# Attention in a two-layer backbone step: order of transposes and value products, and the split of PSUM banks between them

## The chip, the cores and the metric

The kernel runs on 1 core of one Trainium2 chip. The metric is device time of one execution in microseconds; the median of three runs is given, with the lowest and the highest. TensorE is called PE in the profile, its weight loads PEld, VectorE DVE, ScalarE ACT, GpSimd POOL, and SP issues DMAs.

## The reference

One inference step of a backbone with two layers works on 1024 latent tokens (a grid 64 wide) and 256 context tokens of 1024 channels. Layer 0 has neighbourhood attention (8 heads of 64) beside a pooling mixer, layer 1 windowed attention with grouped keys (16 query heads, 4 key heads) and a learned sink per head; each layer ends in a SwiGLU mixer. Cut to the windowed attention:

```python
qb = (q * hd ** -0.5).reshape(bsz, nb, C_BLOCK, hkv, g, hd)
s_nb = jnp.einsum('bnqkgd,bnjkd->bnkgqj', qb, kband)        # 3 blocks of 128 keys, banded
s_nb = jnp.where(valid, s_nb, NEG_INF)
s_ctx = jnp.einsum('bnqkgd,bpkd->bnkgqp', qb, k_ctx)        # 512 cached context keys
p = jax.nn.softmax(jnp.concatenate([sl, s_ctx, s_nb], axis=-1), axis=-1)   # sl: the sink
out = (jnp.einsum('bnkgqp,bpkd->bnqkgd', p[..., 1:1 + n_ctx], v_ctx)
       + jnp.einsum('bnkgqj,bnjkd->bnqkgd', p[..., 1 + n_ctx:], vband))
```

The neighbourhood attention has the same form with a learned bias per offset in place of the band, and no sink. Context tokens attend densely to the 256 context tokens.

## The kernel before, in words

The attention of both layers is one function, `attention` (from L619), called once per layer. Its work is a list of units. A unit is one head and 128 queries with all their keys: 896 keys in layer 0, 896 or 768 in layer 1 (the first and the last block of queries has one block of keys fewer). Units come in pairs a, a+1: the two heads that share a 128-row tile of queries and keys. Per head pair there are eight such long pairs and, after the fourth, one short pair for the context tokens (512 columns: two blocks of 128 queries with 256 keys each). Layer 0 has 4 head pairs, layer 1 has 8.

A unit goes through these steps:

- scores (L632, PE): three products per piece of keys for both heads in turn, into `ps_s`, a tile of two PSUM banks, of which there are two;
- `least` (DVE, L646, or L640 to L643 for short units): adds bias or mask, takes the minimum of the negated logits, and writes `sP` in SBUF;
- `exps` (ACT, L652 and L660): exponentials and their sum, with one more small one for the sink;
- `total` (DVE, L666 and L667): adds the sink term and takes the reciprocal;
- `normalise` (POOL or DVE, L674): scales `sP`;
- `transposes` (PE, L684): 128x128 blocks of `sP` into `ps_t`, four to a bank, so two groups for a long unit;
- `evacuate` (ACT L689 or DVE L691): each group from PSUM to `sT` (`sR` for short units);
- `values` (PE, L700): `sT` times V for both heads side by side, into one bank of `ps_o`;
- `out`: `mix_out` splits the output into a high part (ACT, L1346) and then a low part (DVE, L1348), after which the bank of `ps_o` is free.

PSUM has eight banks here: four for `ps_s`, two for `ps_t`, two for `ps_o`.

The order is written by a planner, `Order`, before anything is emitted. All PE steps are chained by `in_turn`, so PE runs them in just the order in which the loop at the end of `attention` adds them. The steps of the other engines are placed by a greedy list schedule with written costs: among the steps whose predecessors are planned it takes the one that could start earliest, and between equal starts the one of lower class. `least`, `exps` and `total` have class 0, `normalise` and `evacuate` 1, the bias tiles and the two halves of `out` 2. Where a step may go on two engines, it takes the one on which it would end first. A step that takes a slot (`s`, `t`, `o`, `P`, `T`, `R` for the tiles above) can only be planned when a slot has been given back. What the planner emits is fixed: each engine then works through its queue in that order.

DMA loads of keys, queries and values, and some background work, are emitted with the scores.

Of the kernel before, what the change touches and what calls it, by code (L numbers as in the profile page):

```python
# [9 lines left out]
F32 = mybir.dt.float32  # L10
# [113 lines left out]
def hybrid_step(ctx: ExitStack, tc: tile.TileContext, I: dict, O: list):  # L124
# [494 lines left out]
    def attention(p, us, NP, NT, NR, NB, lag, early, spare, bias_ns, lead):  # L619
        psS, c1 = attn_psum  # L620
        NU = len(us)
        S, P, M, T, B, PO = {}, {}, {}, {}, {}, {}
# [53 lines left out]
        def transposes(u, lo, hi):  # L676
            nb = us[u].nb
            if lo == 0:
                T[u] = (p.tile([128, 896], F32, name="sT", bufs=NT) if nb == 1 else
                        p.tile([128, 512], F32, name="sR", bufs=NR))  # L680
            pt = T[u, lo] = psS.tile([128, 512], F32, name="ps_t", bufs=2)
            for i in range(lo, hi):
                j = i // nb + us[u].n // 128 // nb * (i % nb)
                pe.transpose(pt[:, 128 * (i - lo):128 * (i - lo) + 128], P[u][:, 128 * j:128 * j + 128], ident)  # L684

        def evacuate(u, lo, hi, e):
            o, i = T[u][:, 128 * lo:128 * hi], T.pop((u, lo))[:, 0:128 * (hi - lo)]
            if e is act:
                act.activation(o, i, AF.Copy)  # L689
            else:  # L690
                dve.tensor_copy(o, i)  # L691

        def values(a, b, j0, j1, last):
            if j0 == 0:
                PO[a] = psS.tile([128, 512], F32, name="ps_o", bufs=2)
            v = [us[u].vs() for u in (a, b)]
            w = 128 * us[a].nb
            for j in range(j0, j1):
                for h, u in enumerate((a, b)):
                    pe.matmul(PO[a][64 * h:64 * h + 64, 0:w], v[h][j], T[u][:, w * j:w * j + w],  # L700
                              start=(j == 0), stop=(j == len(v[0]) - 1))
            if last:
                T.pop(a), T.pop(b)

        o = Order(lag, s=2, b=NB, P=NP, t=2, T=NT, R=NR, o=2)
        tail = [None]
        ev, ready, queue = {}, {}, []

        def in_turn(on, emit, after, take=(), give=()):
            r = tail[0] = o.add((0, 0), {pe: on}, emit, list(after) + ([tail[0]] if tail[0] else []), take, give)  # L710
            return r

        def issue(a):
            g = us[a]
            n, nb = g.n, g.nb
            own = g.bias is not None and g.sink is None
            sc = in_turn(n * 15 // 11 + 170, lambda e: scores(a), [], ["s", "s"])
            for u in (a, a + 1):
                g, on = us[u], []
                if own:  # L720
                    on = [o.add((2, u), {pool: bias_ns}, lambda e, u=u, g=g: B.update({u: g.bias()}), take=["b"])]
                elif g.bias is not None:
                    B[u] = g.bias()
                here = ["P"] if g.bias is not None else []
                on = o.add((0, u), {dve: n * 11 // 10 + 200}, lambda e, u=u: least(u), [sc] + on, here,
                           (["b"] if own else []) + (["s"] if here else []))
                on = o.add((0, u), {act: n * 5 // 6 + 200 + 144 * (nb - 1) + (0 if g.sink is None else 190)}, lambda e, u=u: exps(u),
                           [on], [] if here else ["P"], [] if here else ["s"])
                on = o.add((0, u), {dve: 160 if g.sink is None else 250}, lambda e, u=u: total(u), [on])
                ready[u] = o.add((1, u), {dve: n * 11 // 20 + 60 * nb} if u < early else  # L730
                                 {pool: n + lead * nb, dve: n * 11 // 20 + spare * nb}, lambda e, u=u: normalise(u, e), [on])

        def turn(u):
            nch = us[u].n // 128
            ev[u] = []
            for lo in range(0, nch, 4):
                hi = min(lo + 4, nch)
                w = 128 * (hi - lo)
                tr = in_turn(107 * (hi - lo) + 30, lambda e, lo=lo, hi=hi: transposes(u, lo, hi), [ready[u]],
                             ["t"] if lo else ["TR"[us[u].nb - 1], "t"], ["P"] if hi == nch else [])  # L740
                ev[u].append(o.add((1, u), {act: 50 + w * 5 // 6, dve: 64 + w * 21 // 20},
                                   lambda e, lo=lo, hi=hi: evacuate(u, lo, hi, e), [tr], give=["t"]))

        def combine(a):
            b, nb, nj = a + 1, us[a].nb, us[a].n // 128 // us[a].nb
            cuts = [0, 4, nj] if nj > 4 else [0, nj]
            for j0, j1 in zip(cuts, cuts[1:]):
                last = j1 == nj
                pv = in_turn((5 + 215 * nb) * (j1 - j0) + 80, lambda e, j0=j0, j1=j1, last=last: values(a, b, j0, j1, last),
                             ev[a] + ev[b], [] if j0 else ["o"], ["TR"[nb - 1]] * 2 if last else [])  # L750
            hi = o.add((2, b), {act: 50 + 110 * nb}, lambda e: us[a].out(0, PO[a]), [pv])
            o.add((2, b), {dve: 70 + 130 * nb}, lambda e: us[a].out(1, PO.pop(a)), [hi], give=["o"])

        for a in range(0, NU + 6, 2):
            if a < NU:
                issue(a)
            if 2 <= a < NU + 2:
                turn(a - 2)
            if 4 <= a < NU + 4:
                combine(a - 4)  # L760
            if 2 <= a < NU + 2:
                turn(a - 1)
        o.run()


# [371 lines left out]
    for ti in (1, 2):  # L1137
        o, n = TB[ti]
# [275 lines left out]
    for hp in range(4):  # L1414
# [28 lines left out]
        for h in range(2):  # L1443
# [10 lines left out]
            us_p.append(Unit(2 * PROMPT, segs, vs, out, nb=2))  # L1454
        us += interleave(us_l, us_p)
    attention(p, us, 4, 4, 2, 3, 80, 3, 1000, 950, 100)
    bg.flush()
    attn_psum[1]()
# [99 lines left out]
    for gi, size in enumerate((4, 2, 2, 2, 2)):  # L1558
# [3 lines left out]
        for ti in range(3):  # L1562
            for (kind, i), (wi, w) in zip(grp, ws):
                pt = ps_tile()
# [44 lines left out]
    for c in range(8):  # L1609
# [27 lines left out]
        for h in range(2):  # L1637
# [10 lines left out]
            us_p.append(Unit(2 * PROMPT, segs, vs, out, nb=2, sink=lambda h=h, c=c: sinkt[:, 2 * c + h:2 * c + h + 1]))  # L1648
        us += interleave(us_l, us_p)
    attention(p, us, 6, 4, 2, 0, 80, 3, 1000, 450, 100)  # L1650
    bg.flush()
    attn_psum[1]()
# [69 lines left out]
```

## Time and profile before

| | us |
|---|---|
| median of 3 runs | 3088.11 |
| lowest, highest | 3081.44, 3091.46 |
| profiled execution | 3094.04 |
| its span, first to last instruction | 3092.3 |
| PE busy | 2937.8 (95%) |
| PEld, DVE, ACT, POOL busy | 2489.7, 1875.6, 1089.3, 822.8 |
| granted PE clock, mean | 0.975 of full speed |

The attention of layer 0 lies at about 298 to 495 us of the span, that of layer 1 at 1728 to 2072. The rest is dense products. An engine's busy time says how long it worked and not whether anything waited for it; a wait is read from the start of an instruction and from the releaser that the trace puts beside it.

### The profile page before, as it was taken

The numbers are of one execution on the slowest core, as the hardware profiler recorded it, in microseconds if no ns is written. First come the engines' busy times: TensorE is split into PE (matmuls) and PEld (weight loads), VectorE is DVE, ScalarE is ACT, GpSimd is POOL, SyncE is SP. The second block draws the span as 40 slices with busy tenths as digits, with TensorE's granted clock in tenths as the row PEclk, the third lists the DMA queues.
The fourth block names the chain that finished last, engine by engine and source line by source line (L and its number), as shares of the span: only waits on it lengthen the run. The fifth ranks groups of instructions, "written<-read, shape, count | busy, mean of one in ns | idle before, by whom it ended". The sixth has DMA issues, their size and how long they took to land.

```text
span 3092.3 us, 46174 instructions
## 1 busy us (share of the span) xinstructions
PE 2937.8 (95%) x18074; PEld 2489.7 (81%) x18074; DVE 1875.6 (61%) x3035; ACT 1089.3 (35%) x2084; POOL 822.8 (27%) x692
## 2 busy tenths in 40 slices
PE   6999999988999999899999999999789999999998
PEld 4878777867888887788878777878678888888887
DVE  5654665577777776544455688862767555554334
ACT  4233773343333332000332577761433333330002
POOL 0241542232333332000222344431323333320002
PEclk9999999989999999999999999999899999999999
DMA  6467644213434436543133410123033223255421
GB/s 248 146 194 228 154 128 154 89 49 129 136 127 130 133 126 237 203 172 138 68 122 141 154 59 31 36 83 99 24 130 116 92 93 101 102 180 204 177 102 69
DMA packets 184330, 394.55 MB, mean 128 GB/s; under 512 B 32176, under 2 KB 69424, under 8 KB 177840
## 3 DMA queue, kind: packets, MB, share of 16 engines
q1 hardware_dynamic: 180656, 385.34, 36.7%
q0 software_dynamic: 3456, 6.26, 0.8%
q8 instruction: 143, 2.34, 0.3%
q14 instruction: 75, 0.61, 0.1%
HBM read 274.32 MB, written 118.23 MB: 127 GB/s over the span
## 4 chain that ended last, share of the span: by engine, by line
PE 68%; DVE 11%; ACT 5%; issue 3%; POOL 3%; DMA 2%; SPq 0%; DVEq 0%; ACTq 0%; POOLq 0%
PE psd L1063 6%; PE psd L1065 6%; PE psd L1064 6%; PE psd L307 6%; PE psd L309 6%; PE psd L308 6%; PE psd L884 6%; PE psd L885 6%; PE psd L886 6%; PE ps_t L684 5%; PE ps_o L700 5%; PE ps_s L632 4%; DVE nacc L388 2%; ACT whl L280 2%; DVE whl L282 2%
## 5 line engine op out<-in xcount | busy, mean ns | idle before, releaser
L308 PE MATMUL psd<-A,whl 128*128 128x256 f32 (+1 forms) x1760 | 585.9, 333 | 16.0 <-DVE A L490 15.0
L307 PE MATMUL psd<-A,whl 128*128 128x256 f32 (+1 forms) x1760 | 588.9, 335 | 7.3 <-ACT A L454 2.7
L309 PE MATMUL psd<-A,whl 128*128 128x256 f32 (+1 forms) x1760 | 583.1, 331 | 2.0 <-DVE whl L282 2.0
L280 ACT ACTIVATE whl<-wraw 128x1024 fp32r<-128x1024 f32 x178 | 187.1, 1055 | 649.7 <-PE psd L1065 461.2
L1063 PE MATMUL psd<-A,whl 128*128 128x512 f32 (+1 forms) x1056 | 378.1, 358 | 16.3 <-DVE x L1067 10.3
L308 PEld LDWEIGHTS psd<-A,whl 128*128 128x128 f32 x1760 | 341.6, 194 | 52.5 <-DVE A L490 17.5
L1064 PE MATMUL psd<-A,whl 128*128 128x512 f32 (+1 forms) x1056 | 376.1, 356 | 0.0
L1065 PE MATMUL psd<-A,whl 128*128 128x512 f32 (+1 forms) x1056 | 376.0, 356 | 0.0
L307 PEld LDWEIGHTS psd<-A,whl 128*128 128x128 f32 x1760 | 342.2, 194 | 41.3 <-ACT A L454 3.2
L309 PEld LDWEIGHTS psd<-A,whl 128*128 128x128 f32 x1760 | 346.0, 197 | 31.7 <-DVE whl L282 3.3
L1067 DVE SCALAR_TENSOR_TENSOR x<-psd,modv,x 128x512 f32<-128x512 f32 (+1 forms) x288 | 186.9, 660 | 283.1 <-PE psd L1065 278.8
L282 DVE TENSOR_TENSOR whl<-wraw,whl 128x1024 fp32r<-128x1024 f32 x174 | 238.7, 1374 | 145.4 <-ACT whl L280 143.3
L884 PE MATMUL psd<-A,whl 128*128 128x512 f32 x704 | 277.4, 394 | 0.0
L885 PE MATMUL psd<-A,whl 128*128 128x512 f32 x704 | 275.4, 391 | 0.0
L886 PE MATMUL psd<-A,whl 128*128 128x512 f32 x704 | 275.4, 391 | 0.0
L674 POOL TENSOR_SCALAR sP<-sP,sm 128x896 f32<-128x896 f32 (+2 forms) x206 | 179.4, 875 | 245.8 <-DVE sm L667 120.0
L1063 PEld LDWEIGHTS psd<-A,whl 128*128 128x128 f32 x1056 | 201.1, 190 | 45.5 <-DVE x L1067 11.1
L1065 PEld LDWEIGHTS psd<-A,whl 128*128 128x128 f32 x1056 | 202.1, 191 | 28.0
L1064 PEld LDWEIGHTS psd<-A,whl 128*128 128x128 f32 x1056 | 201.1, 190 | 27.6
L684 PE MATMUL ps_t<-ident,sP 128*128 128x128 f32 x1408 | 206.6, 285 | 7.3 <-POOL sP L674 2.6
L426 POOL TENSOR_TENSOR nacc<-nacc,ec 128x512 f32<-128x512 f32 (+1 forms) x32 | 34.7, 1084 | 623.2 <-ACT ec L425 621.8
L684 PEld LDWEIGHTS ps_t<-ident,sP 128*128 128x128 f32 x1408 | 152.8, 143 | 57.3 <-issue 24.5
(224 smaller groups left out, 5246.6 us busy)
## 6 DMA issues: line engine op xcount, KB each, us to landing
hd<-x SPq DMA_DIRECT2D x84, 512.0 KB, 3.1
A<-hd SPq DMA_DIRECT2D x20, 2048.0 KB, 12.3
wraw<-in_w_gu_dram SPq DMA_DIRECT2D x60, 512.0 KB, 3.6
st<-in_w_mod_dram SPq DMA_DIRECT2D x112, 256.0 KB, 2.8
wraw<-in_w_down_dram SPq DMA_DIRECT2D x44, 512.0 KB, 3.7
wrawx<-in_w_gu_dram SPq DMA_DIRECT2D x28, 512.0 KB, 3.7
A<-hd SPq DMA_DIRECT2D x14, 1024.0 KB, 14.8
wmod<-in_w_mod_dram SPq DMA_DIRECT2D x48, 256.0 KB, 3.0
```

The lines of the kernel that those rows point to most:

```text
L280: act.activation(h[:, 0], src, AF.Copy)
L282: eng.tensor_tensor(h[:, 1], src, h[:, 0].bitcast(F32), op=OP.subtract)
L307: pe.matmul(ps[:, :n], wh, A[ti].part(0, k), start=(k == 0), stop=False)
L308: pe.matmul(ps[:, :n], wh, A[ti].part(1, k), start=False, stop=False)
L309: pe.matmul(ps[:, :n], wl, A[ti].part(0, k), start=False, stop=(k == 7))
L684: pe.transpose(pt[:, 128 * (i - lo):128 * (i - lo) + 128], P[u][:, 128 * j:128 * j + 128], ident)
L884: pe.matmul(pt, wh, t(0, c), start=(c == 0), stop=False)
L885: pe.matmul(pt, wh, t(1, c), start=False, stop=False)
L886: pe.matmul(pt, wl, t(0, c), start=False, stop=(c == 3))
L1063: pe.matmul(pt[:, :n], wh, t[:, 0, k], start=(k == 0), stop=False)
L1064: pe.matmul(pt[:, :n], wh, t[:, 1, k], start=False, stop=False)
L1065: pe.matmul(pt[:, :n], wl, t[:, 0, k], start=False, stop=(k == nk - 1))
```

## The change

The loop that adds the steps puts the transposes of both heads of a pair side by side and the value products after them. Before, the value products stood between the two heads' transposes. With it `ps_t` gets three banks in place of two and `ps_o` one in place of two; the planner is told the same numbers.

```diff
-            pt = T[u, lo] = psS.tile([128, 512], F32, name="ps_t", bufs=2)
+            pt = T[u, lo] = psS.tile([128, 512], F32, name="ps_t", bufs=3)
...
-                PO[a] = psS.tile([128, 512], F32, name="ps_o", bufs=2)
+                PO[a] = psS.tile([128, 512], F32, name="ps_o", bufs=1)
...
-        o = Order(lag, s=2, b=NB, P=NP, t=2, T=NT, R=NR, o=2)
+        o = Order(lag, s=2, b=NB, P=NP, t=3, T=NT, R=NR, o=1)
...
         for a in range(0, NU + 6, 2):
             if a < NU:
                 issue(a)
             if 2 <= a < NU + 2:
                 turn(a - 2)
+                turn(a - 1)
             if 4 <= a < NU + 4:
                 combine(a - 4)
-            if 2 <= a < NU + 2:
-                turn(a - 1)
         o.run()
```

## Rows read from the trace of the kernel before

**Rows 1.** The page: an engine's busy us, share, instructions; then the chain by engine.
```profile
PE 2937.8 (95%) x18074; PEld 2489.7 (81%) x18074; DVE 1875.6 (61%) x3035; ACT 1089.3 (35%) x2084; POOL 822.8 (27%) x692
...
PE 68%; DVE 11%; ACT 5%; issue 3%; POOL 3%; DMA 2%; SPq 0%; DVEq 0%; ACTq 0%; POOLq 0%
```

**Rows 2.** Busy time by stretch: start:end, us, engines, granted clock, DMA share, GB/s.
```profile
core 0: us, PE busy (x) PEld busy (x) DVE busy (x) ACT busy (x) POOL busy (x), PEclk, DMA share, GB/s
337.60:341.00 3.40, 3.40 (x29) 3.07 (x30) 0.27 (x1) 0.10 (x1) 0.94 (x1) 0.50 0.02 5
443.15:448.10 4.95, 4.95 (x56) 4.05 (x55) 3.57 (x9) 4.05 (x9) 2.88 (x4) 1.00 0.02 3
1811.80:1854.08 42.28, 41.90 (x449) 33.67 (x449) 34.62 (x96) 32.93 (x90) 17.67 (x21) 1.00 0.19 77
1825.56:1844.08 18.52, 18.39 (x192) 14.45 (x192) 15.76 (x43) 13.76 (x39) 7.94 (x10) 1.00 0.00 1
```

**Rows 3.** Timeline, weight loads of layer 1: start, us, engine, line, count [idle before <-releaser].
```profile
1818.56 1.29 PEld L700 LDWEIGHTS ps_o<-sT,V 128*64 128x64 f32 x24 [0.16 <-issue]
...
1825.56 1.17 PEld L632 LDWEIGHTS ps_s<-Ka,Qa 64*128 64x128 f32 x12 [0.17 <-DVE sm L666]
...
1826.98 0.75 PEld L684 LDWEIGHTS ps_t<-ident,sP 128*128 128x128 f32 x7 [0.25 <-POOL sP L674]
...
1827.89 1.51 PEld L700 LDWEIGHTS ps_o<-sT,V 128*64 128x64 f32 x28 [0.17 <-issue]
...
1829.57 0.75 PEld L684 LDWEIGHTS ps_t<-ident,sP 128*128 128x128 f32 x7 [0.17 <-issue]
...
1830.49 0.77 PEld L632 LDWEIGHTS ps_s<-Ka,Qa 64*128 64x128 f32 x12 [0.17 <-DVE sm L667]
```

**Rows 4.** Timeline, from scores to the second head's normalisation; a 768-key pair first.
```profile
1811.80 1.11 PEld L632 LDWEIGHTS ps_s<-Ka,Qa 64*128 64x128 f32 x12 [0.17 <-issue]
...
1817.65 0.91 POOL L674 TENSOR_SCALAR sP<-sP,sm 128x768 f32<-128x768 f32 x1 [0.39 <-DVE A L1348]
...
1820.83 1.51 PE L632 MATMUL ps_s<-Ka,Qa 64*128 64x512 f32 x12
...
1823.56 1.15 DVE L646 CUSTOM_DVE_ANT_0 sP<-ps_s,maskc,sinkt 128x896 f32<-128x896 f32 x1
...
1825.10 0.27 ACT L1346 ACTIVATE A<-ps_o 128x128 fp32r<-128x128 f32 x1
...
1825.44 1.05 ACT L660 ACTIVATE sP<-sP,sm 128x896 f32<-128x896 f32 x1
...
1827.20 1.01 POOL L674 TENSOR_SCALAR sP<-sP,sm 128x896 f32<-128x896 f32 x1 [0.39 <-DVE A L1348]
```

**Rows 5.** Timeline, ACT: an evacuation ahead of the second head's exponentials.
```profile
1801.78 0.59 ACT L689 ACTIVATE sT<-ps_t 128x512 f32<-128x512 f32 x1
...
1802.25 0.30 ACT L652 ACTIVATE sm<-sinkt,sm 128x1 f32<-128x1 f32 x1
```

**Rows 6.** Timeline near short pairs of layer 1.
```profile
1799.86 1.08 PE L700 MATMUL ps_o<-sR,V 128*64 128x256 f32 x8
...
1831.64 0.67 DVE L640 TENSOR_REDUCE sm<-ps_s 128x2 f32<-128x512 f32 x1
...
1832.48 1.75 PE L700 MATMUL ps_o<-sT,V 128*64 128x128 f32 x28
...
1834.97 0.27 DVE L1348 TENSOR_TENSOR A<-ps_o,A 128x128 fp32r<-128x128 f32 x1
...
1836.95 0.42 PEld L684 LDWEIGHTS ps_t<-ident,sP 128*128 128x128 f32 x4 [0.25 <-POOL sP L674]
```

**Rows 7.** DVE's evacuations in layer 1 by tile: count, ns min/median/max, first and last start.
```profile
L691 DVE COPY sT<-ps_t x88: 411/670/692, 1735.5 to 2069.8; 128x512 f32<-128x512 f32 x46, 128x384 f32<-128x384 f32 x32, 128x256 f32<-128x256 f32 x10
```

**Rows 8.** Timeline of layer 0, from scores to the second head's normalisation.
```profile
441.73 1.49 PE L632 MATMUL ps_s<-Kb,Qb 64*128 64x512 f32 x12
...
447.30 1.02 POOL L674 TENSOR_SCALAR sP<-sP,sm 128x896 f32<-128x896 f32 x1 [0.81 <-DVE sm L667]
```

**Rows 9.** Timeline of layer 0, PE: value products that wait, first and last of four.
```profile
337.60 1.98 PE L700 MATMUL ps_o<-sT,Vc 128*64 128x128 f32 x16 [3.08 <-DVE A L1348]
...
479.94 1.09 PE L700 MATMUL ps_o<-sT,Vc 128*64 128x128 f32 x16 [2.17 <-DVE A L1348]
```

## The prediction

> **What bounds the kernel now.** I read the page first: TensorE is busy 95% of the span, and the chain that ended last runs 68% through it [rows 1]. The change touches the attention alone, so the next view is the busy time by stretch [rows 2]. One head pair of the second layer lasts 42.28 us with TensorE busy for 41.90, one long unit pair of the first layer 4.95 with 4.95. In the attention, then, an engine other than TensorE matters only where it makes TensorE wait.
>
> The timeline of weight loads shows what one unit pair costs [rows 3]. Scores (S), transposes of one head (T), products with V (V) and transposes of the other head start at 1825.56, 1826.98, 1827.89, 1829.57, and the next scores at 1830.49: 1.42, 0.91, 1.68 and 0.92 us, 4.93 together. Within a group one load follows another at 0.107 (0.75 over 7) or 0.054 (1.51 over 28). Between groups the loads stop for 0.17, and for 0.25 before the first transposes. Four such gaps stand in a pair.
>
> Last I followed the second head's chain, since the change moves its transposes. Its scores start at 1820.83, its POOL normalisation ends at 1827.20 + 1.01: 7.38 later [rows 4]. Its transposes start today at 1829.57, so the data is 1.36 early. V, which stands ahead of these transposes, is that cover.
>
> **The change, part by part.**
>
> *One change of shape goes.* Two heads' transposes back to back need no gap between them, and V is left by one gap: 0.17 per unit pair. There are 4 x 9 pairs in the first layer and 8 x 9 in the second: 108 x 0.17 = 18.4 us, if TensorE waits for nothing new. No instruction is added or dropped on any engine, and no DMA moves: the loads are issued with the scores, whose place stays.
>
> *The second head's transposes come earlier.* In a pair of two 896-key units TensorE could now start them 1.42 + 0.75 into the frame after their own scores, at 4.76 + 2.17 = 6.93 after these scores. The data comes at 7.38 by the row. Two things in ScalarE's queue shift that. The output copy between the two exponentials (0.27, it sets them back by 0.24) leaves, because V ends later. In its place comes the evacuation of the first four transposes of the second head, which are now there when the first exponential ends: by the planner's rule the earliest start goes first, and its costs, from which I take the order alone and no time, put the evacuation at 3911 after the scores' start and the second exponential at 3921. Where an evacuation already stands between two exponentials, the second starts 0.47 later [rows 5]. I take 7.38 - 0.24 + 0.49 = 7.63 for such pairs, 7.69 with the hop to TensorE. Bounds: 7.14 (no evacuation there) and, with both, 7.9.
>
> V and the next scores are queued behind the waiting transposes, so the loop runs over two pairs: chain, T, V, and then scores again. It takes 7.69 + 0.91 + 1.68 = 10.28 per two pairs, 5.14 each instead of 4.93; without the evacuation 4.9, no gain. A 768-key pair has 6.76 for the chain (scores at 1811.80, normalised at 1817.65 + 0.91, [rows 4]) and does not wait; its scores take 1.28 (1.11 + 0.17), its V 1.46 (1.29 + 0.17, [rows 3]), its six transposes 0.64 and 0.81 with a gap.
>
> Going through the five pairs of a head pair that don't stand near the short unit pair: 4.76 + 5.52 + 4.41 + 4.33 + 5.73 = 24.75. (Where the chain ends late: 7.69 - 4.76 + 0.91 + 1.68 = 5.52 and 7.69 - 4.33 + 0.91 + 1.46 = 5.73. Else scores 1.42 or 1.28, T twice with one gap, V.) Before they take 42.28 - 18.52 = 23.76 [rows 2]. So +0.99.
>
> *One bank for outputs.* V may start only when VectorE's copy of the previous V's output is done. In the plan this copy has the lowest class, so whatever else could start on VectorE at the same moment goes first. In the long run of equal pairs it finds a hole. Near the short pair it does not: the copy now at 1834.97 stands 3.33 behind the first reduction of the short units, and the next V, at 1832.48, ran only because it had the other bank [rows 6]. Now it waits.
>
> First place, V in the frame after the short scores. From the scores of the last long pair: these reductions follow the second head's total, at about 6.5. The same queue, 3.33, one more evacuation of 0.69 (the longest on VectorE, [rows 7]) and the copy itself, 0.27, end at 10.8. V could have started at 7.69 + 0.91 = 8.6: a wait of 2.2. Second place, the short pair's own V. Ahead of the copy stand two reductions (the second ends 3.88 after the scores' start, [rows 4]), an evacuation of 0.69, a total of 0.4, an evacuation of about 0.55, then the copy: 5.8, against 4.0 for the end of the transposes (7.2 - 4.12 + 0.91; the chain of 7.14 and the hop): a wait of 1.9.
>
> The four frames from the last long pair on are then 4.76, 7.77 (10.85 + 1.68 - 4.76), 4.12 (1.42 + 0.42 + 0.59 + 1.68; four transposes are 0.42, [rows 6]) and 6.92 (5.9 + V of the short pair, 1.0, [rows 6]): 23.57 for the 18.52 of before, +5.05. Bounds for the two waits: 0 (the copies find holes) and twice 2.2, and after each up to 1.7 of half clock, as in the first layer below.
>
> *Three banks for transposes.* The fourth group in a row needs the first group's bank. That group is evacuated at once, because ScalarE is free until the first exponential. With the wait ahead of the second head its evacuation is over by then: 0. Bounds 0 and 0.5 (one evacuation) a pair, hidden under the wait for the second head's data.
>
> *First layer.* No sink term there: the second head is ready 6.59 after its scores (441.73 to 448.32, [rows 8]). With the evacuation 7.08, with the hop 7.14: (7.14 + 0.91 + 1.68) / 2 = 4.86 for the 4.95 of now, with seven such pairs in four head pairs -2.3. Here V already waits for the copy, once per head pair: 3.08 to 3.20 three times, 2.17 the last, 11.6 together [rows 9]. With one bank the wait comes one V sooner, behind the same queue as in the second place above: copy done at 5.4, transposes at 3.9, 1.5 each: -5.6. After that wait TensorE has a granted clock of 0.50 (1.2 GHz) for 3.40 us [rows 2], 1.7 lost; half the wait, and I take half of that: -3.4. Bounds for the layer: -25 (no wait left) and +12 (a second one per head pair).
>
> **Sum.** Second layer 8 x (0.99 + 5.05) = +48; first layer -11; together +37 on the profiled execution of 3094.0 (span 3092.3 and 1.7 around it): 3131. The median of the runs is 5.9 under that: **3125 us**, 1.2% slower.
>
> **The rivals.**
>
> *Only the gap counts: faster.* All 18.4 us come through: 3070. It decides if the second head's chain is done within 6.93 of its scores, 0.45 sooner than the row, and each copy within the three groups between two Vs. For it: VectorE is busy 82% of a head pair (34.62 of 42.28) and ScalarE 78% (32.93, [rows 2]), so there is room. Against: the 7.38 is mostly a chain of latencies that room doesn't shorten. The Trainium skill, TensorEngine Tiling (Array Packing), section Key Properties, says that changing the tiling mode drains TensorE; by that alone, with three changes in place of four, this rival is the result. The trace agrees on the gap: 0.17 at each change of shape. Chance 0.12.
>
> *Only the chain counts: within the noise.* VectorE's order lets the copies through, and the second head's wait remains. The four frames near the short pair are 4.76, 5.52, 4.12 and 5.0, +0.9; 8 x (0.99 + 0.9) - 11 = +4: 3092. For it: the two ties in the plan are decided by few nanoseconds of its costs. Against: the copy stands late in the trace of before already. Chance 0.2.
>
> *The waits are paid twice: slower still.* Each of the sixteen waits of about 2 us is followed by half clock as the 2.17 and 3.2 ones in the first layer are, 16 x 1.7 = 27, and the first layer gives nothing back (+11): 3163. Against: the second layer's granted clock is 1.00 throughout now. Chance 0.15.
>
> *The clock falls in longer runs of transposes.* Two heads' transposes, 1.66 a pair, at half clock would cost 1.66 x 108 = 179: 3267. The rows speak against it: at 1.00 through 42.28 us in which a third of TensorE's time is transposes. The Trainium skill, TensorE: Matmul & The Clock Gate, section Part 4: PE-mode transpose, says that such work doesn't count as activity for the clock; by that rule runs twice as long are this rival. Chance 0.05.
>
> My forecast has the remaining 0.48. A difference under 0.3%, 9 us, can't be told from no change here. Faster than that: the first rival and a small part of the second, 0.15. Within: most of the second, 0.17. Slower: 0.68. The range 3080 to 3160 leaves out the first rival, a part of the second, the fourth and the upper half of the third. The likeliest case by itself reaches from 3105 to 3145.
>
> **What would show it.** In the trace after: loads in one run of 14 transposes, with one gap of 0.17 less per pair. TensorE waiting at the second head's transposes for the POOL normalisation in the second layer, some 0.5 to 0.8 where 896-key pairs follow each other. TensorE waiting for the output copy on VectorE at about two Vs per head pair in the second layer, one in the first. An evacuation between the two exponentials. I am wrong if the waits for the output copy sum to under 10 us in the second layer, or if its head pair lasts under 44 us.

## The result and the profile after

The changed kernel takes 3161.41 us (median; 3158.65 to 3167.29) where the kernel before, beside it on the same chip, takes 3089.4: a ratio of 1.0242 (95% interval 1.0227 to 1.0257), 2.4% slower. The forecast had 3125 and a range of 3080 to 3160, so the result lies just outside it. The direction was right and the size was half of what came.

The page of the changed kernel, busy time of each engine and then the chain by engine; the profiled execution took 3158.65 us with a span of 3156.9.

```profile
PE 2946.4 (93%) x18074; PEld 2492.0 (79%) x18074; DVE 1864.8 (59%) x3038; ACT 1083.7 (34%) x2057; POOL 847.5 (27%) x716
...
PE 66%; DVE 13%; ACT 8%; issue 5%; DMA 4%; POOL 4%; SPq 0%; ACTq 0%; DVEq 0%; POOLq 0%
```

Beside [rows 1]: the same 18,074 matmuls, only 8.6 us more busy, but two points less of a longer span. So most of the loss is time in which TensorE waits. VectorE and ScalarE have each gained two to three points on the chain.

The windows of busy time say where. First the whole attention of the second layer before, from its first scores to its first dense product:

```profile
1727.65:2073.14 345.49, 337.04 (x3585) 270.04 (x3584) 278.99 (x767) 267.18 (x716) 138.60 (x157) 1.00 0.14 52
```

The same stretch after, ahead of it a head pair of the first layer, and behind it one head pair of the second and a short piece of that (columns as in [rows 2]):

```profile
340.01:384.90 44.89, 42.96 (x462) 34.43 (x461) 28.79 (x71) 32.33 (x75) 31.69 (x36) 1.00 0.52 121
1714.75:2141.06 426.31, 357.21 (x3586) 281.88 (x3585) 281.75 (x773) 270.43 (x710) 138.48 (x157) 0.95 0.12 42
1816.05:1867.93 51.88, 43.76 (x451) 34.78 (x449) 35.08 (x97) 33.27 (x88) 17.65 (x21) 0.97 0.16 61
1843.20:1848.00 4.80, 4.77 (x41) 3.96 (x42) 0.50 (x3) 0.28 (x1) 1.25 (x3) 0.64 0.00 0
```

The second layer's attention grew by 80.8 us, from 345.5 to 426.3; TensorE is idle for 60.6 of it and busy for 20.2 (357.21 for 337.04, with the same instructions, at a granted clock of 0.95 for 1.00). Its head pair, 42.28 before [rows 2], now lasts 51.88 in this row; five in a row have starts from 1816.05 to 2081.49, 53.1 each. The first layer's attention shrank by 5.6, from 197.3 (298.12 to 495.38) to 191.6 (293.95 to 485.58). Together that is +75.2, against 64.6 between the two profiled executions and 72.0 between the medians. The profiled execution of before lies 4.6 above the median of its runs and that of after 2.8 below; the 10.6 between 75.2 and 64.6 lie in code that both kernels share (4.2 ahead of the first attention, 3.1 between the two, 3.3 behind the second) and were not followed.

What TensorE's weight loads wait for in the second layer's attention, 1714.75 to 2141.06 (us in total, times, longest):

```profile
PEld ps_o L700 <- DVE A L1347: 46.4, 24, 2.2
PEld ps_t L684 <- POOL sP L674: 37.5, 57, 1.2
...
PEld ps_t L684 <- ACT sT L689: 8.2, 30, 0.6
```

Before, the first of these rows is not there: no product with V waited for an output copy in this layer. Now 24 do: three in each head pair but the first, which has two, and one at the end of the layer. (A kernel line after the change stands one lower than before it where it is behind line 758: the copy's L1348 of before is L1347 here.) The second row was 17.7 us before (1730 to 2074), also over 57 waits, 0.31 each and so little more than the usual stop of 0.25 behind the scores [rows 3]. The 20 us on top are data that arrive late for the second head's transposes.

The timeline of TensorE in one head pair after:

```profile
1827.13 0.98 PE L684 MATMUL ps_t<-ident,sP 128*128 128x128 f32 x7 [0.23 <-POOL sP L674]
1828.54 0.98 PE L684 MATMUL ps_t<-ident,sP 128*128 128x128 f32 x7 [0.42 <-POOL sP L674]
1831.16 1.53 PE L700 MATMUL ps_o<-sT,V 128*64 128x128 f32 x24 [1.64 <-DVE A L1347]
...
1834.04 1.95 PE L684 MATMUL ps_t<-ident,sP 128*128 128x128 f32 x14
...
1840.32 0.98 PE L684 MATMUL ps_t<-ident,sP 128*128 128x128 f32 x7 [0.71 <-POOL sP L674]
1843.23 2.92 PE L700 MATMUL ps_o<-sT,V 128*64 128x128 f32 x28 [1.93 <-DVE A L1347]
1846.08 1.93 PE L632 MATMUL ps_s<-Ka,Qa 64*128 64x512 f32 x12
...
1856.60 1.08 PE L700 MATMUL ps_o<-sR,V 128*64 128x256 f32 x8 [1.64 <-DVE A L1347]
```

Three things stand in it. Second heads wait 0.42 to 0.71 for POOL, as forecast. The products with V wait three times: 1.93 behind the short scores and 1.64 at the short pair, the two places of the forecast (2.2 and 1.9), and 1.64 at 1831.16, a place that the forecast did not have. And the V products at 1843.23 take 2.92 where the same 28 took 1.75 before [rows 6]: the stretch 1843.20 to 1848.00 has a granted clock of 0.64.

VectorE's queue ahead of the two copies at 1830.83 and 1842.90 shows why they are late:

```profile
1828.31 1.15 DVE L646 CUSTOM_DVE_ANT_0 sP<-ps_s,maskc,sinkt 128x896 f32<-128x896 f32 x1
...
1829.38 0.69 DVE L691 COPY sT<-ps_t 128x512 f32<-128x512 f32 x1
...
1830.37 0.54 DVE L691 COPY sT<-ps_t 128x384 f32<-128x384 f32 x1
1830.83 0.28 DVE L1347 TENSOR_TENSOR A<-ps_o,A 128x128 fp32r<-128x128 f32 x1
...
1840.45 0.68 DVE L640 TENSOR_REDUCE sm<-ps_s 128x2 f32<-128x512 f32 x1
...
1841.58 0.55 DVE L691 COPY sT<-ps_t 128x384 f32<-128x384 f32 x1
...
1842.31 0.67 DVE L691 COPY sT<-ps_t 128x512 f32<-128x512 f32 x1
1842.90 0.28 DVE L1347 TENSOR_TENSOR A<-ps_o,A 128x128 fp32r<-128x128 f32 x1
```

In both places everything that VectorE can start goes ahead of the copy: in the first `least` of the next pair and two evacuations of the transposes just made, in the second the short units' reductions and two evacuations. The other half of the output, which ScalarE copies, was through long before, for the first at 1826.84, for the second at 1838.83:

```profile
1838.56 0.27 ACT L1345 ACTIVATE A<-ps_o 128x128 fp32r<-128x128 f32 x1
...
1860.86 1.04 ACT L660 ACTIVATE sP<-sP,sm 128x896 f32<-128x896 f32 x1
...
1861.89 0.59 ACT L689 ACTIVATE sT<-ps_t 128x512 f32<-128x512 f32 x1
1862.37 0.30 ACT L652 ACTIVATE sm<-sinkt,sm 128x1 f32<-128x1 f32 x1
```

The last three rows, also ScalarE's, are the second tie of the forecast: an evacuation (1861.89) stands between the exponentials of the two heads.

The weight loads of an equal pair, after:

```profile
1859.05 1.19 PEld L684 LDWEIGHTS ps_t<-ident,sP 128*128 128x128 f32 x11 [0.26 <-issue]
1860.46 0.31 PEld L684 LDWEIGHTS ps_t<-ident,sP 128*128 128x128 f32 x3 [0.22 <-ACT sT L689]
1860.93 1.51 PEld L700 LDWEIGHTS ps_o<-sT,V 128*64 128x64 f32 x28 [0.17 <-issue]
```

No gap separates the heads: the seven of one run into four of the next. The gap that the change saves, 0.17 [rows 3], is there. But the fourth group, the last three transposes, then waits 0.22 for its bank, and the saving is gone.

### The profile page after: what moved, and what is told of

Read it like the earlier page. It is cut to its first block, busy times and chain, and to the rows that moved or that the text cites. A ratio compares the mean times of both kernels' runs of the same rounds, so it can differ in the third digit from the quotient of the medians.

```text
span 3156.9 us, 46045 instructions
## 1 busy us (share of the span) xinstructions
PE 2946.4 (93%) x18074; PEld 2492.0 (79%) x18074; DVE 1864.8 (59%) x3038; ACT 1083.7 (34%) x2057; POOL 847.5 (27%) x716
## 4 chain that ended last, share of the span: by engine, by line
PE 66%; DVE 13%; ACT 8%; issue 5%; DMA 4%; POOL 4%; SPq 0%; ACTq 0%; DVEq 0%; POOLq 0%
PE psd L307 7%; PE psd L309 7%; PE psd L308 7%; PE psd L1062 6%; PE psd L1063 6%; PE psd L1064 6%; PE psd L885 5%; PE psd L884 5%; PE psd L883 5%; PE ps_o L700 4%; PE ps_s L632 3%; PE ps_t L684 3%; ACT sP L660 2%; DVE nacc L388 2%; ACT whl L280 2%
## 5 line engine op out<-in xcount | busy, mean ns | idle before, releaser
L674 POOL TENSOR_SCALAR sP<-sP,sm 128x896 f32<-128x896 f32 (+2 forms) x230 | 203.7, 889 | 309.6 <-DVE sm L667 212.4
L684 PE MATMUL ps_t<-ident,sP 128*128 128x128 f32 x1408 | 199.9, 283 | 30.3 <-POOL sP L674 27.1
```

## The experiments

The table orders the runs by what they tell. "Head pairs" is the time in the second layer from the start of the first product with V of a short pair to the start of the last such product, which is seven head pairs and some 0.7 us (for the first layer three: 144.2 before, 139.1 after).

| kernel | median us | ratio to before, 95% | second layer, seven head pairs |
|---|---|---|---|
| before | 3089.4 | 1 | 296.7 |
| after | 3161.41 | 1.0242 (1.0227 to 1.0257) | 371.6 |
| order only | 3122.24 | 1.0099 (1.0076 to 1.0121) | 325.2 |
| banks only | 3155.27 | 1.0214 (1.0190 to 1.0238) | 346.3 |
| after, copies first | 3126.56 | 1.0117 (1.0095 to 1.0138) | 334.8 |
| after, exponentials first | 3124.52 | 1.0126 (1.0110 to 1.0141) | 339.2 |
| after, copies and exponentials first | 3094.78 | 1.0032 (1.0022 to 1.0043) | 312.2 |
| after, copies first, one normalisation left out | 3091.58 | 1.0018 (1.0008 to 1.0027) | 305.4 |
| after, copies first, one pair deeper | 3087.21 | 1.0007 (0.9997 to 1.0016) | 300.6 |
| the same, groups of 3 and 4 | 3085.12 | 0.9987 (0.9977 to 0.9998) | 296.2 |
| after, waits filled | 3148.73 | 1.0207 (1.0190 to 1.0224) | 360.2 |
| before, copies first | 3080.34 | 0.9968 (0.9957 to 0.9980) | 302.4 |
| before, copies first in the first layer | 3067.55 | 0.9945 (0.9932 to 0.9957) | 296.8 |
| both layers at their best | 3072.12 | 0.9953 (0.9940 to 0.9967) | 296.3 |

The kernels ran on several chips, so differences of a point or less are taken between ratios.

### The two parts, each alone

The new order with the old banks (e1_order_only), against the kernel after:

```
-            pt = T[u, lo] = psS.tile([128, 512], F32, name="ps_t", bufs=3)
+            pt = T[u, lo] = psS.tile([128, 512], F32, name="ps_t", bufs=2)
-                PO[a] = psS.tile([128, 512], F32, name="ps_o", bufs=1)
+                PO[a] = psS.tile([128, 512], F32, name="ps_o", bufs=2)
-        o = Order(lag, s=2, b=NB, P=NP, t=3, T=NT, R=NR, o=1)
+        o = Order(lag, s=2, b=NB, P=NP, t=2, T=NT, R=NR, o=2)
```

> The new order with the old banks (2 and 2). Theory M (the single output bank is the larger part of the loss): the 24 waits of V for the output copy in the second layer (41 us, and the half clock behind some of them) go; new waits of some 0.5 to 0.7 us come at the third group of transposes, which now needs the first group's bank, in most of 108 pairs: 3120 to 3150. Rival R (the order alone, by the second head's normalisation, makes the loss, whatever the banks): no better than 3150.

The old order with the new banks (e2_banks_only), against the kernel after:

```
                 turn(a - 2)
-                turn(a - 1)
             if 4 <= a < NU + 4:
                 combine(a - 4)
+            if 2 <= a < NU + 2:
+                turn(a - 1)
```

> The old order with the new banks (3 and 1). M: V of the second layer waits for the output copy at one to three places of each head pair, about 2 us each, as in the changed kernel: 3115 to 3150. R: the old order hides the copy as it hides the normalisation, so 3080 to 3095.

Measured: 3122.24 and 3155.27, the second a few us above the range expected. Waits of TensorE's products between 1730 and 2030 with the order alone, and one of them in the timeline:

```profile
PE ps_t L684 <- ACT sT L689: 24.1, 44, 0.8
PE ps_t L684 <- POOL sP L674: 7.0, 13, 1.5
...
1833.49 0.95 PE L684 MATMUL ps_t<-ident,sP 128*128 128x128 f32 x7 [0.51 <-ACT sT L689]
```

Banks alone, waits of the weight loads:

```profile
PEld ps_o L700 <- DVE A L1348: 35.6, 12, 3.0
```

The order alone loses as was expected of it. With two banks the third group of transposes needs the bank of the first, and the second head waits for that evacuation, here 44 times in 300 us and in the first layer 28 times (14.3 us). The weight loads' list puts these waits down to POOL (34.8 us, 51 times), but the normalisation in the pair shown runs from 1831.94 for 1.01, and ends half a us before the transposes start. So this run does not give the price of the second head's late data. The waits for the output copy are gone with the second output bank.

The single output bank makes V wait for VectorE's copy with no help from the order: 12 waits of 3.0 on average in these 300 us. Alone the two parts cost 0.99 and 2.14 points, together 2.42. They need not add, since the order alone has a wait that the third bank takes away. Much of the difference lies in the first layer: its three head pairs take 144.2 with the order alone, 151.2 with the banks alone and 139.1 with both.

### The rank of the output copies

In the kernel after, both output copies move from the lowest class of the plan to the first (e3_after_copy_first):

```
-            hi = o.add((2, b), {act: 50 + 110 * nb}, lambda e: us[a].out(0, PO[a]), [pv])
-            o.add((2, b), {dve: 70 + 130 * nb}, lambda e: us[a].out(1, PO.pop(a)), [hi], give=["o"])
+            hi = o.add((0, b), {act: 50 + 110 * nb}, lambda e: us[a].out(0, PO[a]), [pv])
+            o.add((0, b), {dve: 70 + 130 * nb}, lambda e: us[a].out(1, PO.pop(a)), [hi], give=["o"])
```

> The changed kernel with the output copies in the plan's first class in place of its last. M (one bank hurts because the plan lets everything else go ahead of the copy): nearly all waits for the output copy go, the second head's waits stay: a head pair of the second layer falls from 51.9 to about 45, the kernel to 3095 to 3115. Rival (one bank is too few whatever the plan does): over 3140.

The same edit in the kernel before (e4_before_copy_first):

> The kernel before with the output copies in the plan's first class. M: the four waits of V in the first layer (11.6 us) and the half clock behind them (up to 1.7 each) go, nothing else moves: 3070 to 3078. Rival (these four waits come from something else, or the copies delay the chain as much as they gain): 3085 or more.

Measured: 3126.56, outside what was expected, and 3080.34, a little above it. In the first the waits for the copy are gone; this is the row that is now the largest between 1730 and 2030 (26.1 us over 40 waits after):

```profile
PEld ps_t L684 <- POOL sP L674: 43.0, 65, 2.2
```

Half of the loss went, 1.25 points, but TensorE now waits longer for the second head, because the copies stand ahead of that head's chain. In one pair of this kernel an evacuation and the output copy lie between the two exponentials (1850.96 and 1853.07, 2.11 apart), the second head's total comes behind a `least`, and its transposes wait 1.92 (1856.81). V products behind such a wait run at half clock in part (28 in 3.06 at 1809.84): the granted clock over the 300 us is still 0.97. In the kernel before, the edit shows both what such a rank gives and what it takes. The first layer's three head pairs fall from 144.2 to 132.0, because there V waited for this copy already [rows 9]. The second layer's seven rise from 296.7 to 302.4, because there nothing waited for it. Hence the kernel before with the edit in the first layer alone (e11_before_copy_first_l0):

```
+            hi = o.add((0 if NB else 2, b), {act: 50 + 110 * nb}, lambda e: us[a].out(0, PO[a]), [pv])
+            o.add((0 if NB else 2, b), {dve: 70 + 130 * nb}, lambda e: us[a].out(1, PO.pop(a)), [hi], give=["o"])
```

> The kernel before with the output copies in the first class in the first layer alone. With them first in both layers a head pair of the first layer fell from 47.5 to 43.5 and one of the second rose from 42.3 to 43.1. If these add without each other: 3089 less 16, 3069 to 3075. Rival: the first layer's gain is lost in what follows it (weights that are not yet loaded): 3080 or more.

Measured: 3067.55, a little under the range expected and 0.55% under before, with 132.0 and 296.8 for the two distances. It is the fastest of all these kernels.

### What is left when the copies are out of the way

The copies first, and in the second layer the normalisation of the second head of each pair is left out (e5_no_second_norm):

```
+            if NB == 0 and u % 2:
+                return
```

> As the kernel with the copies first (3126), and the second head's normalisation is left out in the second layer (its products with V are not scaled). Theory P (what is left there is the second head's normalisation, 57 us of waits of the weight loads): a head pair of the second layer falls from 48.0 to 41 to 43, the kernel to 3075 to 3090. Rival (the waits are a queue's doing and move to the exponentials or the evacuations): over 3105.

Measured: 3091.58, just above the range expected. Waits between 1730 and 2030 (POOL is now the first head's normalisation alone; the line numbers are two higher):

```profile
PEld ps_t L686 <- POOL sP L676: 16.0, 34, 0.8
PEld ps_t L686 <- ACT sT L691: 13.6, 55, 0.3
```

So the chain of the second head holds most of what remained, 0.99 of 1.17 points, with the half clock behind its waits (the granted clock is 1.00 here), and the bank of the fourth group comes up from behind it: 55 waits of 0.25.

Then the second tie by itself. The planner's cost of the exponentials is raised by 60, so that they go ahead of an evacuation that could start at the same time; with the copies first (e7_exps_first), and in the kernel after as it is (e9_exps_first_alone):

```
-                on = o.add((0, u), {act: n * 5 // 6 + 200 + 144 * (nb - 1) + (0 if g.sink is None else 190)}, lambda e, u=u: exps(u),
+                on = o.add((0, u), {act: n * 5 // 6 + 260 + 144 * (nb - 1) + (0 if g.sink is None else 190)}, lambda e, u=u: exps(u),
```

> As the kernel with the copies first (3126), and the plan's cost of an exponential is 60 higher, so that the second head's exponential comes ahead of the evacuation at the tie. Theory P2 (the evacuation between the exponentials makes the second head 0.5 late): a head pair of the second layer falls from 48.0 to 45 to 46.5, the kernel to 3110 to 3118. Rival (the chain is late by its own latencies, and the evacuation comes later instead): 3122 or more.

> The changed kernel (3161) with the plan's cost of an exponential 60 higher and nothing else, so that the second head's exponential goes ahead of the evacuation; the output copies keep the last class. With the copies first this edit gave 32 us (3126.6 to 3094.8). Theory A (the two losses add): 3125 to 3140, and the waits for the output copy stay, 30 us or more in the second layer. Rival (an earlier chain lets the copy through as well, both losses have one root in the plan): under 3110, with few waits for the copy.

Measured: 3094.78, better than expected, and 3124.52, at the lower edge of what was expected if the two edits add (3125, and 30 us or more of waits for the copy in the second layer, where 29.0 were measured). ScalarE's timeline with both edits:

```profile
1858.97 1.04 ACT L660 ACTIVATE sP<-sP,sm 128x896 f32<-128x896 f32 x1
...
1859.99 0.29 ACT L652 ACTIVATE sm<-sinkt,sm 128x1 f32<-128x1 f32 x1
1860.18 1.03 ACT L660 ACTIVATE sP<-sP,sm 128x896 f32<-128x896 f32 x1
```

The exponentials follow at 1.21 (1858.97, 1860.18) where 1.69 lay between them after (1860.86 to 1862.55). With the exponentials alone, waits between 1730 and 2030:

```profile
PEld ps_t L684 <- POOL sP L674: 27.6, 56, 0.7
PEld ps_o L700 <- DVE A L1347: 22.5, 12, 1.9
```

The waits for the copy fall from 17 to 12 in 300 us: the one behind the short scores is gone (V at 1832.41 follows the transposes at once), as the plan of VectorE shifts with that of ScalarE, and the granted clock rises from 0.95 to 0.99. The second head's own wait falls where the evacuation had stood between the exponentials, from 0.71 to 0.43 and from 0.49 to 0.20, and stays at 0.42 elsewhere. So this edit takes away parts of both losses, and the rival that they have one root in the plan holds in part. By the ratios the copies' rank is worth 1.25 points alone and 0.94 on top, the exponentials' 1.16 alone and 0.85 on top; together 2.10 of the 2.42.

Next the rest. The copies first, and in the second layer both the transposes and V one unit pair later, so that the chain has a pair more to run (e8_deeper; NP >= 6 picks the second layer, and the loop runs one pair longer):

```
+        far = 4 if NP >= 6 else 2
...
+            if far <= a < NU + far:
+                turn(a - far)
+                turn(a - far + 1)
+            if far + 2 <= a < NU + far + 2:
+                combine(a - far - 2)
```

> As the kernel with the copies first (3126), and in the second layer transposes and value products come one pair later, so the second head's chain has a whole pair more of time. Theory P: the waits for the normalisation go, 57 us of the weight loads' idle time there; a head pair falls to 41 to 43, the kernel to 3075 to 3090. Rival (VectorE or ScalarE can't serve a pair in less than 47 us by head pair in this order, or three banks for transposes are too few): over 3105.

Measured: 3087.21, as expected. The waits for POOL are gone from the head of the list, and the bank of the fourth group leads it:

```profile
PEld ps_t L684 <- ACT sT L689: 14.5, 56, 0.9
```

Then the same with groups of three and four transposes in place of four and three (e10_deeper_3_then_4), so that the first bank comes free sooner:

```
-            for lo in range(0, nch, 4):
-                hi = min(lo + 4, nch)
+            for lo, hi in {7: ((0, 3), (3, 7)), 6: ((0, 3), (3, 6))}.get(nch if NP >= 6 else 0) or [
+                    (lo, min(lo + 4, nch)) for lo in range(0, nch, 4)]:
```

> As the kernel one pair deeper (3087), and in the second layer a head's first group has 3 transposes and its second 4 in place of 4 and 3, so that the first group is evacuated sooner and in less time, and the fourth group's bank is free some 0.1 us sooner by its start. Theory B (what is left of the saved gap goes into the wait of the fourth group for its bank, 14.5 us in 300): this wait falls to half or less, a head pair from 42.9 to 41.8 to 42.4, the kernel to 3079 to 3084. Rival (another engine sets the pace there): no change, 3086 to 3089.

```profile
PEld ps_t L684 <- ACT sT L689: 3.3, 15, 0.2
```

Measured: 3085.12, a little above what was expected, with the bank's wait down from 14.5 to 3.3. The weight loads now show nearly what the change wants:

```profile
1809.11 0.31 PEld L684 LDWEIGHTS ps_t<-ident,sP 128*128 128x128 f32 x3 [0.22 <-ACT sT L689]
...
1821.38 1.61 PEld L684 LDWEIGHTS ps_t<-ident,sP 128*128 128x128 f32 x14
1823.15 1.51 PEld L700 LDWEIGHTS ps_o<-sT,V 128*64 128x64 f32 x28 [0.17 <-DVE sm L666]
```

Fourteen transposes stand in one run, with V behind them. The run takes 1.61 where 14 loads at 0.107 [rows 3] are 1.50 and where it took 1.72 in the kernel after, so half of the pause for the fourth group's bank is left; with 768 keys, the first row, the fourth group still waits 0.22. The seven head pairs take 296.2, against 296.7 before. The largest wait left there is one per head pair for a short unit's exponentials, 5.9 us over 7 waits between 1730 and 2030.

Last, the first layer as in e4_before_copy_first and the second as here (e12_both_layers):

```
+            pt = T[u, lo] = psS.tile([128, 512], F32, name="ps_t", bufs=3 if NP >= 6 else 2)
...
+                PO[a] = psS.tile([128, 512], F32, name="ps_o", bufs=1 if NP >= 6 else 2)
...
+            if far <= a < NU + far:
+                turn(a - far)
+                if far == 4:
+                    turn(a - far + 1)
+            if far + 2 <= a < NU + far + 2:
+                combine(a - far - 2)
+            if far == 2 and 2 <= a < NU + 2:
                 turn(a - 1)
```

> First layer as in the kernel before with the copies first (43.4 us per head pair), second layer as in the kernel one pair deeper with groups of 3 and 4 (42.2 per head pair, against 42.3 in the kernel before). Theory: once its waits are mended, the new order in the second layer is worth what the old one is, so this one lands beside the kernel before with the copies first in the first layer alone, 3064 to 3071. Rival (the saved gap still comes through in the whole): under 3062.

Measured: 3072.12, just above what was expected, and no better than the 3067.55 of the small edit to the kernel before (intervals 0.9940 to 0.9967 and 0.9932 to 0.9957). With both its waits mended, the new order is worth no more than the old one here.

### The clock after the waits

In the kernel after, the last group of the second head's transposes is repeated, five times in all, ahead of the products that wait (e6_fill_waits). The extra transposes write the same tile again:

```
-            for i in range(lo, hi):
+            again = 5 if NB == 0 and u % 2 and u // 2 % 9 in (1, 3, 5) and hi == us[u].n // 128 else 1
+            for i in again * list(range(lo, hi)):
```

> The changed kernel (3161), in the second layer with the last three transposes ahead of each V that waits for the output copy done five times over (the same values to the same place, 1.3 us of TensorE work inside the waits of 1.6 to 1.9). Theory K (behind these waits TensorE runs at half clock, which costs some 15 to 20 us in the second layer): the granted clock there rises from 0.95 to 0.99 or more, and the kernel falls by 8 to 20 us, to 3141 to 3153. Rival (the clock falls for another reason, or the copies wait for these transposes): 3158 or more.

Measured: 3148.73, as expected; with more work the kernel is 13 us faster by the medians, 11 by the ratios. A window of this kernel, its granted clock 1.00 where that of the kernel after is 0.95:

```profile
1730.00:2030.00 300.00, 269.85 (x2838) 218.56 (x2836) 202.85 (x563) 193.44 (x513) 104.00 (x118) 1.00 0.10 37
```

Its timeline at the third frame (VectorE, then TensorE) and behind the short scores:

```profile
1831.47 0.56 DVE L692 COPY sT<-ps_t 128x384 f32<-128x384 f32 x1 [0.42 <-PE ps_t L685]
1832.28 1.53 PE L701 MATMUL ps_o<-sT,V 128*64 128x128 f32 x24 [0.85 <-DVE A L1348]
...
1841.46 2.29 PE L685 MATMUL ps_t<-ident,sP 128*128 128x128 f32 x19 [0.70 <-POOL sP L674]
1844.38 1.75 PE L701 MATMUL ps_o<-sT,V 128*64 128x128 f32 x28 [0.62 <-DVE A L1348]
```

Behind the short scores the idle time ahead of V is 0.62 in place of 1.93, V takes 1.75 in place of 2.92, and the granted clock over the 300 us is 1.00 in place of 0.95. So TensorE's half clock behind the waits is a part of the loss, and 11 to 13 us are what is left of it after the price of the extra work. That price is not nothing. At the other two places VectorE's last evacuation waits for the extra transposes (0.42 in the first row), and the copy stands behind it: the frames there, from one pair's scores to the next's, last 7.75 and 7.49 where they last 7.22 and 6.97 in the kernel after, 1.05 per head pair and about 8 us in all. With it the half clock comes to 19 to 21 us, and TensorE's busy time in the kernel after, 20.2 us more for the same instructions, says the same.

## Why the prediction was right in direction and short in size

The step that failed is the second layer's term of the sum: "Second layer 8 x (0.99 + 5.05) = +48". It measured +80.8. In the forecast's own frames, one per unit pair from 1816.05 on, each from one pair's scores to the next's, a head pair was to take 4.41, 4.33, 5.73, 4.76, 7.77, 4.12, 6.92, 4.76 and 5.52, 48.32 in all. It took 4.69, 4.66, 7.22, 4.98, 8.48, 4.56, 6.97, 5.01 and 5.31, 51.88, and the head pairs with more half clock up to 55.0. Three parts of the term were too small.

- **A third wait for the copy.** "In the long run of equal pairs it finds a hole" is wrong for one frame, the third (1825.40 to 1832.62): 7.22 for 5.73. There `least` of the next pair and two evacuations of the 896-key units just transposed stand ahead of the copy at 1830.83, and V waits 1.64. With 1.49 in seven head pairs (the first has no earlier V at that place) that is 10 us. I had looked for the copy where it was late before; the rule that made it late, lowest class behind whatever can start, holds in every frame, and I should have gone through them all.
- **The fourth group's bank.** "With the wait ahead of the second head its evacuation is over by then: 0." In the pairs that don't wait for the second head there is no such cover. The four frames in question (first, second, fourth, eighth) are 0.28, 0.33, 0.22 and 0.25 longer than forecast; that is 1.08 per head pair, about 9 us. It is within the bound I gave, 0 to 0.5 a pair, and about what the saved gap brings. That the evacuation of the first group is the cause is shown by e10_deeper_3_then_4, where a smaller first group halves the pause in the runs of 14.
- **Half clock behind the waits.** This is the largest part. I had counted it behind the waits of the first layer and left it at nothing in the second, where it stood in a bound and in a rival, because the granted clock was 1.00 there; but before the change no V waited there. It measured about 20 us. In the head pair above it is in the frame behind the short scores and the next: 8.48, where the first head pair of the layer has 7.31 with V at the full rate (1733.65 to 1740.96), and 4.56 for 4.12.

10, 9 and 20 make 39. Against them stand two frames that were forecast too long, 7.77 for the 7.31 at full clock and 5.52 for 5.31, about 5 us in eight head pairs. That leaves 34 for the 32.5 that are missing (80.8 less 48.3); the rest, at the ends of the layer, was not followed.

**What held.** The gap of 0.17 goes, as forecast. The second head's wait is there with 0.42 to 0.71 for the 0.5 to 0.8 of the forecast, but the evacuation between the exponentials is its cause only in part: it stands there in the fifth and the ninth frame, with waits of 0.71 and 0.49, which fall in e9_exps_first_alone (it sets the second exponential back by 0.48, for the 0.49 that I had taken from a row of 0.47). Where the wait is 0.42 nothing stands between the exponentials (1824.34 and 1825.55, 1.21 apart): the two heads are normalised 1.41 apart (1826.06 and 1827.47), and the transposes of the first take less than that. The two waits for the copy that were forecast at 2.2 and 1.9 measured 1.93 and 1.64: 0.3 too long each. The test that I had set (under 10 us of waits for the copy, or a head pair under 44, would prove me wrong) came out at 46.4 and 51.88.

**First layer.** Its head pair was to fall by 2.8 (a quarter of the 11) and fell by 2.6, from 47.50 to 44.89. The layer gave 5.6 and not 11, in part because the last head pair has a wait that I did not have. Two rows of TensorE's timeline there, the earlier the wait for the copy that remains:

```profile
329.01 1.08 PE L700 MATMUL ps_o<-sR,Vp 128*64 128x256 f32 x8 [1.56 <-DVE A L1347]
...
453.99 1.40 PE L684 MATMUL ps_t<-ident,sP 128*128 128x128 f32 x7 [2.35 <-POOL sP L674]
```

Just ahead of the second, from 450.33 to 452.6, ScalarE and VectorE split a weight tile of the next stage (1.06 and 1.23), and the second head's chain stands behind it. That is read from the queue; no run took the split away. The remaining 2 to 3 us of the layer were not followed.

**The rivals.** That only the gap counts fell: 14 transposes in a row bring the gap, and the bank takes it back. That only the chain counts fell with the 46.4 us of waits for the copy. The waits paid twice, at 3163, came nearest to the result, and by its half clock, 27 us for the 20 that came, where I had nothing. The rest of its sum is wrong: 16 waits and no gain in the first layer, where the trace has 24 waits and a gain of 5.6. Its rule, half clock after every such wait, does not hold either: the wait of 1.64 at 1831.16 is followed by V at 1.53 for 24, the full rate. The fourth, a clock that falls in longer runs of transposes, did not happen: 14 in a row take 1.95 at 1834.04 to 1835.92 in the kernel after, and with groups of three and four they stand in the long pairs at a clock of 1.00. The Trainium skill, TensorE: Matmul & The Clock Gate, section Part 4: PE-mode transpose, says that transposes don't count as busy time for the clock in the way matmuls do; here the measurements go against it, since e6_fill_waits put nothing but transposes into the waits and the clock stayed at 1.00.

**What the change is worth without its ties.** The saving of 18.4 us at most came in full in no run. With the copies' rank, a pair more of lead and the smaller first group the second layer's head pairs take 296.2 for 296.7. Nine gaps of 0.17 would make 1.5 per head pair. The pause for the fourth group's bank, 0.11 in six runs of 14 transposes and 0.22 in two of 12, takes 1.1 of it, and one wait for the short units' exponentials, 0.84, takes more than the rest.

## What to carry to other kernels

A buffer count of one makes the release of that buffer a part of the critical path, so whatever releases it has to be ranked by that and not as clean-up: go through every frame of the plan with the rule that orders the queue, not only the frames where it was late before. Before taking work out from between a producer and its consumer, ask what it covered: the V products between the two heads' transposes cost a gap of 0.17 and hid 1.4 of slack and a bank's release. A wait of TensorE can also cost a second time behind it: here half clock added 20 us to 60.6 of idle time. And a rank that frees one wait takes its time from another chain, so set it only where something waits (the first layer here, 0.55% with one condition).

## What was not expected of the hardware

The granted clock fell to half (1.2 GHz) after some waits of TensorE and not after others of the same length, at the same place of different head pairs:

```profile
1739.28 1.75 PE L700 MATMUL ps_o<-sT,V 128*64 128x128 f32 x28 [1.93 <-DVE A L1347]
...
1895.13 3.25 PE L700 MATMUL ps_o<-sT,V 128*64 128x128 f32 x28 [1.93 <-DVE A L1347]
```

Both rows are of the kernel after, with the same products behind the same wait; from 1739.20 to 1741.00 the granted clock is 1.00, from 1895.10 to 1898.40 it is 0.52. What tells the two apart is open. Transposes alone, put into the waits, kept the clock at its full level (1.00 for 0.95 over 300 us) and made a kernel with more work 11 to 13 us faster.
